# FFN1 by seven products from group 2 on, with left operands stored whole

## The chip, the cores and the metric

The kernel runs on one core of a Trainium2 chip. The metric is the device time of one execution in microseconds. Three runs of the kernel before took 1750.65, 1750.65 and 1752.18 us; their median is 1750.65.

## The reference

One layer of a decoder: a half-step feed-forward block, a mixer of a short convolution and a diagonal state-space model (SSM), and a second half-step feed-forward block, each behind an RMSNorm with shift and scale from a condition vector. Tokens and model width are 1024 each, the feed-forward width is 2816; all in float32.

```python
h = modulate(rms_norm(x, ffn1_norm), sh1, sc1)
x = x + 0.5 * g1 * swiglu(h, w_gate, w_up, w_down)      # (silu(h @ w_gate) * (h @ w_up)) @ w_down
h = modulate(rms_norm(x, mix_norm), sh2, sc2)
...                                                     # conv and SSM, joined by w_out, added to x
h = modulate(rms_norm(x, ffn2_norm), sh3, sc3)
x = x + 0.5 * g3 * swiglu(h, w_gate2, w_up2, w_down2)
y = rms_norm(x, final_norm)
```

## The kernel before

**Products.** Activations lie transposed, a tile being 128 features by 512 tokens (half h of the tokens, feature tile k). Each float32 product is made of three passes (`mm3`): both operands are split into a rounded part `hi` and a rest `lo`, and hi x hi, hi x lo, lo x hi are accumulated in a PSUM bank. A split is a cast on ScalarE (ACT) and a subtraction on VectorE (DVE). Weights come from DRAM as raw tiles of 1 MB (`rawp`, two buffers), are split in pairs of half-columns called granules, and lie in a ring of three granule buffers; `ws.take` hands a granule to the products, and `ws.free` starts the split of a later one.

**FFN1.** The 2816 features are 22 tiles, two to a group, so groups 0 to 10. A group's gate and up projections can be made in two ways. By eight products (`gate_up`), each side and feature tile of each token half takes 8 `mm3`, 64 in all or 192 matmuls. By seven products (`seven`, a Strassen-Winograd scheme), the activation is a 2 by 2 block matrix of token halves and feature halves, A11, A12, A21, A22, and the products use the left operands A11, S1, S2, S3, A12, A22 and S4, where S1 = A21 + A22, S2 = S1 - A11, S3 = A11 - A21 and S4 = A12 - S2. Each side takes seven products of four `mm3`, 56 `mm3` or 168 matmuls for a group. For it GpSimd (POOL) combines the weights' blocks with eight additions for a group (`combine`, `split_done`), and VectorE adds the partial results out of PSUM, five additions for each side. `SEVEN_FROM = (4, 1)` says from which group on this is done in FFN1 and in FFN2.

**Left operands of the projections.** `combos` makes S1, S2 and S3 for each of four k from the split parts of the normalised activation: three whole values are put together again (`whole`, f in the profile), one sum and two differences are made, and the three results are split. `combos_last` makes S4 from two more whole values, once the last plain group is done with A21.

**Left operands of the down projection.** The result a = silu(gate) x up of groups 1 to 8 is used by `down7`, again by seven products, in two chunks of four groups. The seven left operands of each group are made at the end of the group, split (`keep`, `keep_sums`, `keep_last`), and stored as hi and lo together, 512 KB each, to DRAM (`kept`). Groups 0, 9 and 10 keep only their four blocks, for plain products at the end (`last_parts`, fald in the profile). `fetch` brings an operand back, hi and lo, into a buffer that the product before has freed: chunk 0 during the up side of the last group by seven (fa10u), chunk 1 during the second half of the first `down7` (`fad0`; a `down7` has two halves p, of seven steps with two banks each), the last blocks during the second half of the second. FFN2 uses the same functions (fb and fbd in the profile), with groups 1 to 8 kept.

**Side work and order.** A `Clock` counts `mm3` calls. Each `period` calls it runs one step of a generator in `clock.side`. In FFN1 that is `side1`: first `ssm_base` (18 steps: the powers and rotors of the SSM), then `combos` (12), then eight `ssm_batch` (tables for four SSM groups each, stored to DRAM and used in the mixer, with `kp` and `tp` on TensorE). The period is 4 in groups 1 to 3 (3 after `combos_last` is put in front) and 7.75 after. At the start of group 10 what is left of the side work is run at once. Apart from the prologue (`InOrder.strict`), the framework lays down the order of each engine's instructions at compile time; each engine then runs its own list in that order, and a wait at its head holds all behind it. All loads and stores are issued by one queue, SP.

**The x tiles.** `xp` holds x (eight tiles of 512 KB) in the prologue; the normalised x goes through temporary tiles into hi and lo, and `xp` is closed after group 0's first products. x is loaded again at the start of group 10.

Of the kernel before, what the change touches and what calls it, by code (L numbers as in the profile page):

```python
# [21 lines left out]
P = 128  # L22
# [12 lines left out]
SEVEN_FROM = (4, 1)  # L35
# [196 lines left out]
def hymba_layer(ctx: ExitStack, tc, x_d, wm1_d, wmod_d, gu1_d, gs1_d, ds1_d, wl1_d, win_d, wout_d, glu_d, gu2_d, gs2_d, wd2_d, ds2_d, wl2_d, cols_d, cond_d, lam_d, bc_d, out_d):  # L232
# [257 lines left out]
    def keep_sums(kept, a11, a21, a22, name):  # L490

        V.tensor_tensor(out=a22[:], in0=a21[:], in1=a22[:], op=ALU.add)
        keep(kept, "S1", a22, name)
        V.tensor_tensor(out=a21[:], in0=a11[:], in1=a21[:], op=ALU.subtract)
        keep(kept, "S3", a21, name)
        V.tensor_tensor(out=a22[:], in0=a22[:], in1=a11[:], op=ALU.subtract)
        keep(kept, "S2", a22, name)

    def keep_last(kept, a12, s2, name):
        V.tensor_tensor(out=a12[:], in0=a12[:], in1=s2[:], op=ALU.subtract)  # L500
        keep(kept, "S4", a12, name)

    def gu_keep(fi, h, pg, pu, afs, kept, name):
        t = t2k(f"{name}{fi}_{h}")
        A.activation(t[:], pg[:], AF.Silu)
        V.tensor_tensor(out=t[:], in0=t[:], in1=pu[:], op=ALU.mult)
        keep(kept, f"A{h + 1}{fi + 1}", t, name)
        afs[fi, h] = t
        if len(afs) == 4 and "S1" in kept:
            keep_sums(kept, afs[0, 0], afs[0, 1], afs[1, 1], name)  # L510
            keep_last(kept, afs[1, 0], afs[1, 1], name)
# [63 lines left out]
    def seven(name, between, place=1, kept=None, then=None):  # L575
# [4 lines left out]
        for side in "gu":  # L580
# [5 lines left out]
            def out(h, fi, t):  # L586
                nm = f"{name}_{fi}_{h}"
                if side == "g":
                    A.activation(t[:], t[:], AF.Silu)
                    gate_[h, fi] = t  # L590
                else:
                    V.tensor_tensor(out=t[:], in0=t[:], in1=gate_[h, fi][:], op=ALU.mult)
                    if kept is None:
                        a_tiles[fi, h] = split_act(t[:], nm + "a")
                    else:
                        keep(kept, f"A{h + 1}{fi + 1}", t, name)

            for n, (left, b) in enumerate(SEVEN):
# [26 lines left out]
                elif n == 4:  # L625
                    t = gate_[0, 0]
                    V.tensor_tensor(out=t[:], in0=t[:], in1=bank["A"][:], op=ALU.mult)
                    if kept is None:
                        a_tiles[0, 0] = split_act(t[:], f"{name}_0_0a")
                    else:  # L630
                        keep(kept, "A11", t, name)
                elif n == 5:
                    add(u3, u3, "E")
                    out(1, 0, u3)
                    if side == "u" and kept is not None and "S1" in kept:
                        keep_sums(kept, gate_[0, 0], u3, t1, name)
                elif n == 6:
                    add(u2, u2, "C")
                    out(0, 1, u2)
                    if side == "u" and kept is not None and "S1" in kept:  # L640
                        keep_last(kept, u2, t1, name)
# [161 lines left out]
    for k in range(KT):  # L803
        ts = []
# [6 lines left out]
        for h in range(2):  # L811
            hi, lo = parts(f"h1{k}_{h}")
            A.activation(hi, ts[h][:], AF.Identity, bias=sh)
            V.scalar_tensor_tensor(out=lo, in0=ts[h][:], scalar=sh, in1=hi.bitcast(F32), op0=ALU.add, op1=ALU.subtract)
# [13 lines left out]
    xp_open.close()  # L828
# [832 lines left out]
```

## Time and profile before

| | before |
|---|---|
| median of three runs | 1750.65 us |
| span of the profiled execution | 1750.3 us |
| FFN1 groups 1 to 3, by eight products | 87.2 to 219.3 us |
| FFN1 groups 4 to 10, by seven | 219.3 to 505.4 us |
| FFN1 down projection by seven | 505.4 to 669 us |
| FFN2 by seven, groups 1 to 10 | 1153 to 1534 us |
| FFN2 down projection by seven | 1534 to 1686 us |

The profile is of one execution. Its span, from the first to the last instruction, is 0.35 us below the median of the runs. Engines are PE (TensorE matmuls), PEld (its weight loads), DVE, ACT, POOL and the queue SPq. Nearly all instructions are recorded at line 107, that of a helper, so they are told apart by their tiles: `w<-raw` is a weight split, `fa4uC` the bank C of the up side of FFN1's group 4, `rot` and `rott` the rotors. In a table by stage, each engine's busy us are followed by the number of its instructions; then come the granted clock of PE, the busy share of the DMA engines and what they moved in GB/s. In a timeline the columns are start, length, what ran, and in brackets how long the engine had been idle and what released it. A wait is given as total, times and longest.

### The profile page before, as it was taken

Reading aid. Unit: us, or ns where it says so; the run is one execution under the profiler, and the core shown is the slowest. Engines: PE = TensorE matmul, PEld = TensorE weight load, DVE = VectorE, ACT = ScalarE, POOL = GpSimd, SP = SyncE. Lnnn points to the kernel's source line nnn. Section 1 sums busy time; section 2 is a strip of 40 time slices with the busy share of each in tenths; the row PEclk is TensorE's granted clock in tenths of the full one; section 3 lists DMA queues with packets and bytes.
Section 4 is the critical chain, followed back from the end, with each engine's and each line's share of the span. In section 5 each row is a group of like instructions: output and inputs, shape, how many; then the busy total and the mean of one; then the engine's idle time right before and its main releaser. Section 6 shows DMA issues by size and latency. Waiting matters only on the chain.

```text
span 1750.3 us, 20808 instructions
## 1 busy us (share of the span) xinstructions
PE 1677.9 (96%) x7532; PEld 1379.6 (79%) x7532; DVE 1300.6 (74%) x2286; ACT 566.0 (32%) x934; POOL 351.1 (20%) x241
## 2 busy tenths in 40 slices
PE   4999999999999999999999899989999999999996
PEld 3788887878787888887877778778888888888886
DVE  7999999999855687744656977967777666676656
ACT  4223234444322221332113424423343443322221
POOL 0000132222222221100000022023323322333211
PEclk9999999999999999999999999999999999999998
DMA  8245544444597877134654450113444334669312
GB/s 319 85 145 196 207 167 165 182 169 178 196 391 266 326 256 292 56 84 149 210 157 140 144 191 25 48 46 135 157 162 173 147 133 156 239 242 366 115 49 96
DMA packets 101080, 304.54 MB, mean 174 GB/s; under 512 B 19057, under 2 KB 34673, under 8 KB 89842
## 3 DMA queue, kind: packets, MB, share of 16 engines
q1 hardware_dynamic: 100978, 303.22, 48.4%
q8 instruction: 59, 0.97, 0.2%
q14 instruction: 43, 0.35, 0.1%
HBM read 212.47 MB, written 86.51 MB: 171 GB/s over the span
## 4 chain that ended last, share of the span: by engine, by line
PE 76%; DVE 14%; DMA 5%; issue 2%; POOL 1%; ACT 1%; SPq 1%; DVEq 0%; POOLq 0%; ACTq 0%
PE wo L107 4%; PE fald L107 3%; DVE w L107 3%; PE p L107 2%; PE fb10d L107 2%; PE fbd_0B L107 2%; PE fbd_1B L107 2%; PE u L107 2%; DMA swz<-si 2%; PE b L107 1%; DVE x L107 1%; PE c L107 1%; PE fa3u L107 1%; PE fb0g L107 1%; PE fa2g L107 1%
## 5 line engine op out<-in xcount | busy, mean ns | idle before, releaser
L107 ACT CAST w<-raw 128x512 fp32r<-128x512 f32 (+1 forms) x358 | 236.2, 689 | 484.3 <-issue 75.0
L107 DVE TENSOR_TENSOR w<-raw,w 128x512 fp32r<-128x512 f32 (+1 forms) x358 | 295.9, 845 | 107.3 <-ACT w L107 106.5
L164 POOL TENSOR_TENSOR sums<-raw 128x512 f32<-128x512 f32 x50 | 71.4, 1429 | 451.5 <-DMA raw<-in_gs 263.3
L173 POOL TENSOR_TENSOR raw<-sums,raw 128x512 f32<-128x512 f32 x50 | 77.7, 1554 | 371.1 <-DVE w L107 358.9
L175 POOL TENSOR_TENSOR raw<-raw 128x512 f32<-128x512 f32 x50 | 77.5, 1549 | 89.6 <-DVE w L107 73.0
L107 DVE CUSTOM_DVE_ANT_0 wm<-wm,cact 128x1024 f32<-128x1024 f32 x56 | 76.6, 1375 | 16.9 <-DMA wm<-in_wmod 16.9
L165 POOL TENSOR_TENSOR raw<-raw 128x512 f32<-128x512 f32 x50 | 77.3, 1547 | 3.2
L366 POOL TENSOR_TENSOR n3aq<-n3aq,n3aq 128x512 f32<-128x512 f32 x5 | 8.3, 1666 | 281.4 <-DMA wm<-in_wmod 255.7
L107 PE MATMUL p<-h,w 128*128 128x512 f32 x192 | 50.0, 423 | 8.0 <-DVE h L107 5.1
L107 DVE TENSOR_TENSOR w<-sums,w 128x512 fp32r<-128x512 f32 x50 | 52.5, 1063 | 3.6 <-ACT w L107 3.0
L107 PEld LDWEIGHTS p<-h,w 128*128 128x128 f32 x192 | 39.4, 207 | 18.4 <-DVE h L107 6.4
L107 PE MATMUL v<-h,w 128*128 128x512 f32 x192 | 46.9, 395 | 0.0
L107 PE MATMUL c<-h,w 128*128 128x512 f32 x192 | 46.6, 395 | 0.0
L107 PE MATMUL wo<-oa,w 128*128 128x512 f32 x192 | 45.6, 392 | 0.9 <-DVE w L107 0.7
L107 PE MATMUL b<-h,w 128*128 128x512 f32 x192 | 45.6, 394 | 0.0
L107 PE MATMUL wo<-ob,w 128*128 128x512 f32 x192 | 45.5, 392 | 0.0
L107 PE MATMUL u<-h,w 128*128 128x512 f32 x192 | 44.7, 392 | 0.2 <-DVE h L107 0.2
L107 PEld LDWEIGHTS wo<-oa,w 128*128 128x128 f32 x192 | 35.8, 188 | 9.0 <-DVE w L107 1.1
L107 PEld LDWEIGHTS u<-h,w 128*128 128x128 f32 x192 | 35.7, 188 | 8.2 <-DVE h L107 0.6
L107 PEld LDWEIGHTS wo<-ob,w 128*128 128x128 f32 x192 | 35.8, 188 | 7.7 <-DVE ob L107 0.4
L107 PEld LDWEIGHTS b<-h,w 128*128 128x128 f32 x192 | 35.6, 188 | 7.1
L107 PEld LDWEIGHTS c<-h,w 128*128 128x128 f32 x192 | 35.4, 188 | 7.0
(1565 smaller groups left out, 4056.2 us busy)
## 6 DMA issues: line engine op xcount, KB each, us to landing
raw<-in_gs SPq DMA_DIRECT2D x34, 1024.0 KB, 5.5
wm<-in_wmod SPq DMA_DIRECT2D x56, 512.0 KB, 5.3
raw<-in_ds SPq DMA_DIRECT2D x16, 1024.0 KB, 7.2
raw<-in_gu SPq DMA_DIRECT2D x10, 1024.0 KB, 7.0
mw<-in_wm SPq DMA_DIRECT2D x8, 1024.0 KB, 12.8
x<-in_x SPq DMA_DIRECT2D x16, 512.0 KB, 8.0
raw<-in_win SPq DMA_DIRECT2D x8, 1024.0 KB, 5.4
raw<-in_wl SPq DMA_DIRECT2D x5, 1024.0 KB, 6.7
```

Source lines behind the costliest of these rows:

```text
L107: r = getattr(self.engine, name)(*args, **kw)
L164: self.G.tensor_tensor(out=f, in0=r[2], in1=r[1], op=ALU.subtract)
L165: self.G.tensor_tensor(out=r[1], in0=r[1], in1=r[0], op=ALU.subtract)
L173: self.G.tensor_tensor(out=r, in0=s["t3"], in1=r, op=ALU.add)
L175: self.G.tensor_tensor(out=r, in0=self.chunk(j, 3), in1=r, op=ALU.subtract)
L366: nc.gpsimd.tensor_tensor(out=a, in0=a, in1=sq[:, :n], op=ALU.add)
```

## The change

1. `SEVEN_FROM` becomes (2, 1): groups 2 and 3 of FFN1 are made by seven products; their weights come in the order and the combinations of that scheme. Group 1 is then the last by eight.
2. The prologue writes the normalised x (before the shift) over x, and `xp` stays open. `combos1` takes the left sums from there, with the shift added on the way, without putting hi and lo together, and closes `xp` after S4. It runs first in `side1`; `ssm_base` and the batches follow. The small pool `first` is opened behind it.
3. `rotors` makes both tables in one pass: the upper 64 partitions hold what was a second table (`baset` is laid out for this), and a negated copy is made on ACT. Two multiplications and an addition in place of four and two; four stores of half size for the two tables.
4. Kept operands are stored whole, not split: two to a tile of 512 KB (`HALVES`), stored when both are written, so four stores for a group instead of seven. `fetch` brings 256 KB back and splits it then, on ACT and DVE. Sums are read from these tiles, and A21 is stored too. This holds for both FFNs.
5. The clock's periods become 3.5 in group 1, 2 after its second last part, and 7 from group 2 on.

```diff
-SEVEN_FROM = (4, 1)
+SEVEN_FROM = (2, 1)
...
-    def keep(kept, left, src, name):
-
-        if left in kept:
-            t = mov(f"{name}{left}")
-            A.copy(t[:, 0, :], src[:])
-            V.tensor_tensor(out=t[:, 1, :], in0=src[:], in1=t[:, 0, :].bitcast(F32), op=ALU.subtract)
-            SP.dma_start(kept[left][:], t[:].bitcast(F32))
...
+    HALVES = dict(A22=("X", 0), A11=("X", 1), A21=("Y", 0), A12=("Y", 1), S1=("Z", 0), S3=("Z", 1), S2=("W", 0), S4=("W", 1))
...
+        def done(self, left):
+            t, i = HALVES[left]
+            self.there.setdefault(t, set()).add(i)
+            if len(self.there[t]) == 2:
+                SP.dma_start(self.dram[t][:], self.tiles[t][:])
...
+    def keep(kept, left, a, b, op, name):
+
+        V.tensor_tensor(out=kept.place(left, name), in0=a, in1=b, op=op)
+        kept.done(left)
...
     def fetch(kept, left, where, name):
         t = mov(f"{name}{left}", where)
-        SP.dma_start(t[:].bitcast(F32), kept[left][:])
-        return t[:, 0, :], t[:, 1, :]
+        hi, lo = t[:, 0, :], t[:, 1, :]
+        whole_ = lo.bitcast(F32)
+        SP.dma_start(whole_, kept.stored(left))
+        A.copy(hi, whole_)
+        V.tensor_tensor(out=lo, in0=whole_, in1=hi.bitcast(F32), op=ALU.subtract)
+        return hi, lo
...
-            ts.append(t2k(f"h1t{k}_{h}"))
-            V.scalar_tensor_tensor(out=ts[h][:], in0=x[k][h], scalar=scl[:, 0, k : k + 1], in1=bcs[h][:], op0=ALU.mult, op1=ALU.mult)
+            V.scalar_tensor_tensor(out=x[k][h], in0=x[k][h], scalar=scl[:, 0, k : k + 1], in1=bcs[h][:], op0=ALU.mult, op1=ALU.mult)
...
-        def rotors(i, op):
-            r, t = bt(f"rot{b}_{i}"), bt(f"rott{b}_{i}")
-            V.tensor_tensor(out=v3(r), in0=st[0], in1=bs[i], op=ALU.mult)
-            V.tensor_tensor(out=v3(t), in0=st[1], in1=bs[1 - i], op=ALU.mult)
+        def rotors():
+
+            r, t = bt(f"rot{b}"), bt(f"rott{b}")
+            V.tensor_tensor(out=v3(r), in0=st[0], in1=bs[0], op=ALU.mult)
+            V.tensor_tensor(out=v3(t), in0=st[1], in1=bs[1], op=ALU.mult)
             yield
-            V.tensor_tensor(out=r[:, :512], in0=r[:, :512], in1=t[:, :512], op=op)
-            SP.dma_start((co_d, si_d)[i][b], r[:, :512])
-
-        yield from rotors(0, ALU.subtract)
+            V.tensor_tensor(out=r[:, :512], in0=r[:, :512], in1=t[:, :512], op=ALU.add)
+            A.activation(t[64:128, :512], r[64:128, :512], AF.Copy, scale=-1.0)
+            for half in (slice(0, 64), slice(64, 128)):
+                SP.dma_start(co_d[b, half], r[0:64, :512])
+            SP.dma_start(si_d[b, 0:64], r[64:128, :512])
+            SP.dma_start(si_d[b, 64:128], t[64:128, :512])
+
+        yield from rotors()
...
+    def combos1():
...
+        for k in range(4):
+            (t11, t21), (t12, t22) = x[k], x[4 + k]
+            V.scalar_tensor_tensor(out=t22, in0=t22, scalar=both[:, k : k + 1], in1=t21, op0=ALU.add, op1=ALU.add)
+            blocks["S1"].append(split_act(t22, f"h1S1_{k}", "B"))
+            yield
+            V.tensor_tensor(out=t21, in0=t11, in1=t21, op=ALU.subtract)
+            blocks["S3"].append(split_act(t21, f"h1S3_{k}", "B"))
+            yield
+            V.scalar_tensor_tensor(out=t11, in0=t22, scalar=sh[:, k : k + 1], in1=t11, op0=ALU.subtract, op1=ALU.subtract)
+            blocks["S2"].append(split_act(t11, f"h1S2_{k}", "B"))
+            yield
+            V.scalar_tensor_tensor(out=t12, in0=t12, scalar=sh[:, 4 + k : 5 + k], in1=t11, op0=ALU.add, op1=ALU.subtract)
+            yield
+        while not left_free:
+            yield
+        for k in range(4):
+            blocks["S4"].append(split_act(x[4 + k][0], f"h1S4_{k}", "A"))
+            yield
+        xp_open.close()
+        first_opened()
+
     def side1():
+        yield from combos1()
+        sb = side_open.enter_context(tc.tile_pool(name="sb", bufs=1, side="right"))
...
-        yield from combos(act1, "h1", "BBB")
         for b in range(NB):
             yield from ssm_batch(b)
...
-    clock.period = 4
+    clock.period = 3.5
...
-    clock.period = 7.75
+    clock.period = 7
```

More of the change, by code (lines that the diff above doesn't have):

```diff
@@ L634, in seven @@
                     out(1, 0, u3)
-                    if side == "u" and kept is not None and "S1" in kept:
-                        keep_sums(kept, gate_[0, 0], u3, t1, name)
+                    if side == "u" and kept is not None and kept.sums:
+                        keep_sums(kept, name)
                 elif n == 6:
@@ L639, in seven @@
                     out(0, 1, u2)
-                    if side == "u" and kept is not None and "S1" in kept:
-                        keep_last(kept, u2, t1, name)
+                    if side == "u" and kept is not None and kept.sums:
+                        keep_last(kept, name)
                 if q % 2:
@@ L827, in hymba_layer @@
     InOrder.strict = False
-    xp_open.close()
     def kept_for(g, all_seven=True):
-        names = [left for left, _ in SEVEN] if all_seven else ["A11", "A12", "A21", "A22"]
-        return {left: scratch.tile([P, 2, HALF], F32, name=f"kept{g}{left}") for left in names}
+        return Kept(f"kept{g}", all_seven)
     kept = {g: kept_for(g, g not in LAST[0]) for g in range(NGRP)}
@@ L1088, in ssm_batch @@
         yield from gate1()
-        yield from rotors(1, ALU.add)
         yield from gate1()
@@ L1160, in gate_up @@
                     if h:
-                        clock.side.appendleft(combos_last(act, "h1", "A"))
-                        clock.period = 3
+                        left_free.append(True)
+                        clock.period = LAST_PERIOD
                 ws.free(2)
```

86 lines of the change are left out of this document (54 added, 32 removed).

## The prediction

> **What bounds the kernel now.** I read the page's shares first, then a table by stage, the chain of waits in order of time, PE's waits, and last the groups of VectorE and the two places where kept operands come back.
>
> ```profile
> PE 1677.9 (96%) x7532; PEld 1379.6 (79%) x7532; DVE 1300.6 (74%) x2286; ACT 566.0 (32%) x934; POOL 351.1 (20%) x241
> DVE  7999999999855687744656977967777666676656
> ```
>
> TensorE (PE) is busy for 96% of the span, so matmuls taken away are time taken away, unless another engine then ends last. VectorE (DVE) is at 74% on average, but at nine tenths in slices 2 to 10, the stage that the change rewrites. By group of FFN1 (groups 1 to 9; first the wall time, then PE, PEld, DVE, ACT, POOL):
>
> ```profile
> core 0: us, PE busy (x) PEld busy (x) DVE busy (x) ACT busy (x) POOL busy (x), PEclk, DMA share, GB/s
> 87.20:130.72 43.52, 43.52 (x193) 36.07 (x193) 41.94 (x222) 12.17 (x17) 0.00 (x0) 1.00 0.43 146
> ...
> 301.04:340.70 39.66, 39.66 (x181) 32.46 (x181) 37.32 (x59) 15.93 (x29) 11.78 (x9) 1.00 0.50 180
> 340.70:385.00 44.30, 41.73 (x183) 33.51 (x182) 41.14 (x62) 16.37 (x31) 14.53 (x9) 0.96 0.48 171
> ...
> sum 380.07, PE 374.19 PEld 306.45 DVE 358.23 ACT 139.94 POOL 83.17; mean PE 41.58 PEld 34.05 DVE 39.80 ACT 15.55 POOL 9.24
> ```
>
> DVE works 358.23 of 380.07 us: two engines are nearly full at once. The chain shows PE's prices (start, length):
>
> ```profile
> 130.72 10.88 PE fa2g L107 x48
> ...
> 185.12 0.98 PE kp L107 x8
> 186.09 0.59 PE tp L107 x4
> ...
> 219.34 2.72 PE fa4gA L107 x12
> ```
>
> A group by eight products is 192 matmuls, four such pieces, 43.52 us; by seven it is 14 pieces of 2.72, 38.08 us. Groups 1 to 9 need 3 x 43.52 + 6 x 38.08 + 8 x 1.57 (kp and tp of each table batch) = 371.6 us. They took 380.07, so 8.5 us are lost, where PE waits for DVE and then runs for a while at a lower clock (0.96 in the row from 340.70):
>
> ```profile
> PE fa7gC L107 <- DVE fa7gt L107: 2.6, 1, 2.6
> PE fa5uC L107 <- DVE fa5ut L107: 2.1, 1, 2.1
> PE fa9gC L107 <- DVE fa9gt L107: 1.2, 1, 1.2
> ```
>
> **The change part by part.** *Groups 2 and 3 by seven products*: 2 x 5.44 = 10.9 us of PE gone. I take all of it, if DVE leaves room, which is the next sum.
>
> ```profile
> L107 DVE TENSOR_TENSOR w<-raw,w 128x512 fp32r<-128x512 f32 x75 | 54.5, 747 | 5.5 <-ACT w L107 5.4
> L107 DVE TENSOR_TENSOR rot<-rot,rott 128x512 f32<-128x512 f32 x16 | 16.0, 1001 | 0.2
> L107 DVE TENSOR_TENSOR rott<-rs,rt 128x512 f32<-128x512 f32 x16 | 15.3, 959 | 2.1 <-DMA co_d<-rot 2.1
> L107 DVE TENSOR_TENSOR rot<-rs,rt 128x512 f32<-128x512 f32 x16 | 14.2, 885 | 0.1
> L107 DVE TENSOR_TENSOR w<-raw,w 128x1024 fp32r<-128x1024 f32 x10 | 12.2, 1218 | 0.0
> L107 DVE TENSOR_TENSOR f<-h 128x512 f32<-128x512 f32 x16 | 10.9, 688 | 0.1
> L107 DVE TENSOR_TENSOR fa1S<-fa,fa1S 128x512 fp32r<-128x512 f32 x4 | 2.8, 689 | 0.0
> L107 DVE TENSOR_TENSOR fa4A<-fa4gc,fa4A 128x512 fp32r<-128x512 f32 x1 | 1.8, 1780 | 0.0
> L107 DVE TENSOR_TENSOR fa4gu<-fa4gt,fa4gB 128x512 f32<-128x512 f32 x1 | 0.7, 669 | 0.0
> ```
>
> DVE in groups 1 to 9: each of the two groups adds 10 additions from PSUM (0.67) and turns 4 wide weight splits (1.22) into 14 narrow ones (0.75): 6.7 + 10.5 - 4.9 = 12.3, so +24.6. The left sums take 4 whole-tile operations for each of four k instead of 9, as the whole values are in x's place: 20 fewer x 0.69 = -13.8. Rotors halved: half of 16.0 + 15.3 + 14.2 = -22.7. Stores kept whole: seven splits fewer in each of groups 1 to 8 and four in group 9, 60 x 0.69 = -41.4. The sum is 358.2 + 24.6 - 13.8 - 22.7 - 41.4 = 305 us in 371.6 - 10.9 = 360.7 us of PE: 85% instead of 94%.
>
> That is an average, so by stage. A group by seven without side work is seen in FFN2:
>
> ```profile
> 1191.35:1229.42 38.07, 38.07 (x169) 31.54 (x169) 26.81 (x40) 15.29 (x27) 11.56 (x8) 1.00 0.42 152
> 1495.98:1534.06 38.08, 38.08 (x170) 31.55 (x169) 21.38 (x30) 13.33 (x23) 12.48 (x9) 1.00 0.74 275
> 1534.06:1572.10 38.04, 38.04 (x170) 31.51 (x169) 27.46 (x35) 10.22 (x18) 11.04 (x8) 1.00 0.62 250
> 1572.10:1610.20 38.10, 38.10 (x170) 31.58 (x169) 25.21 (x34) 9.17 (x16) 10.74 (x8) 1.00 0.86 323
> 1610.20:1648.30 38.10, 38.10 (x170) 31.57 (x169) 25.85 (x31) 9.17 (x16) 14.57 (x10) 1.00 0.44 174
> ```
>
> It has 26.8 us of DVE, 22.0 without its seven splits (7 x 0.69). Group 1 now gets the left sums: 32 operations x 0.69, 8 products and sums x 0.69, some 6 us of weights: 34 of 43.5 us. The period gives 13 + 8 side steps there and the sums need 20, so S4 stands just before group 2. Groups 2 and 3 get the table base: it cost 41.94 less 15 x 0.69 and 5 x 1.22, 25.5 us, in group 1's 16 steps; now 8 steps to a group, 12.8, so 34.8 of 38.1 us, the tightest place. Groups 4 to 9 get 4/3 of a batch each: (37.32 - 26.81 - 2.8 for rotors) x 4/3 = 10.3, so 32.3 of 40.2. Stalls should mostly go; groups 2 and 3 at 91% keep some. Of the 8.5 us I take 5.5 as won (bounds 0 and 8.5).
>
> *Fetching*. A kept operand comes back as 256 KB instead of 512, and ACT's cast and DVE's subtraction now stand behind its landing, 28 of each for a chunk, in both FFNs: a full block of ACT 28 x 0.62 (the casts' price, the same width as the weights') and of DVE 28 x 0.69 = 19.3 us. Behind a cast that waits for its DMA are ACT's weight casts and t1 copies, and PE waits for those weights; behind the subtraction are DVE's bank evacuations. In FFN2 PE has no idle time there at all today. Chunk 0 falls into the last 15 us of group 10 and into the first half (1534 to 1572): 21.4 + 27.5 + 19.3 = 68.2 of 76.1 us, though most of it lands around the seam. Chunk 1 falls into 1572 to 1610: 25.2 + 19.3 = 44.5 us of DVE against 38.1 of PE, 6.4 over, paid back in the next half, which has 12 us free. PE feels it only if a weight or a bank is late. That margin is thin:
>
> ```profile
> 1597.44 0.41 SPq L107 DMA_DIRECT2D raw<-in_ds  x1
> ...
> 1607.21 0.62 ACT L107 CAST w<-raw 128x512 fp32r<-128x512 f32 x1 [1.15 <-DMA raw<-in_ds]
> 1609.08 1.77 DVE L107 TENSOR_TENSOR w<-raw,w 128x512 fp32r<-128x512 f32 x1
> ```
>
> The split at 1609.08 serves a product that starts at 1610.2. Its raw tile landed ten us after issue, in a stage at 323 GB/s: 3.2 MB, 1 MB of it the raw tile itself. Halving the rest saves 1.1 MB, 3.4 us, which pays half of the 6.4. I take +5 us for FFN2, from 0 (backlog absorbed) to +14: 6.4, and 4 at the seam, with the slow clock after each stall.
>
> FFN1 has the same added work, but a loss to win back:
>
> ```profile
> 505.40:543.50 38.10, 38.03 (x168) 31.19 (x166) 23.52 (x35) 8.26 (x15) 2.15 (x3) 1.00 0.93 346
> 543.50:590.00 46.50, 42.71 (x169) 33.85 (x170) 26.76 (x33) 10.18 (x19) 16.66 (x12) 0.93 0.74 281
> 532.98 1.28 SPq L107 DMA_DIRECT2D raw<-in_ds  x2
> 543.07 0.62 ACT L107 CAST w<-raw 128x512 fp32r<-128x512 f32 x1 [14.26 <-DMA raw<-in_ds]
> ```
>
> The half from 543.50 takes 46.50 instead of 38.1, 8.4 lost, because the next weights were issued only at 532.98, behind fetches that fill the queues (share 0.93), and landed ten us later. 28 x 256 KB less is 7.3 MB, 21 us at 346 GB/s, so they come earlier. Against this stands the same +5. I take -2 (bounds -8.4 and +14).
>
> *At nothing*: stores of four 512 KB tiles instead of seven (DMA share is 0.42 to 0.50 there; the tile is held until both its halves are written, and four buffers serve four tiles); the new groups' two copies and narrower casts, and the rotors' negation, on ACT, which works 15.93 of 39.66 us; x written in place. The weight bytes are the same. The rotors' stores are four for each batch instead of two; si's lower half waits on SP for ACT's negation, and behind it on SP are weight loads, which run two tiles ahead. Without that cover it is about 1 us (0.62 and an issue of 0.41) for each of eight batches. The tables move about a group and a half later; the last batch's stores now stand on SP at the end of group 9, ahead of the reload of x, which x's first use, in the seam's half, is 38 us behind; if it came late, the whole of that delay would show at 505.
>
> Sum: -10.9 - 5.5 + 5 - 2 = -13.4 on the profiled execution's 1750.3, so 1736.9; the runs' median is 0.35 above that execution, so **1737 us**.
>
> The row of 1780 ns is a price of its own: the same subtraction takes 0.69 elsewhere, and the slow ones stand where POOL is busy. [...] It speaks against this change, which adds such GpSimd work.
>
> **The rivals.** *A, the fetch costs more than the seven products win.* DVE and ACT stand behind landings in order, and the backlog isn't absorbed: 10.4 us (6.4 and 4) in each FFN, some 13 with the slow clock, and FFN1's relief lost: -16.4 + 26 = +9.6, **1760**. It decides the sign from 8 us for each FFN on. For it: 44.5 against 38.1 us, and a split with 1.1 us to spare. Against: half the bytes, and 12 us free in the next half. 0.2.
>
> *B, DVE becomes the bound of groups 2 and 3.* Each now has eight POOL combinations, as 1191.35 shows, beside the table base. If each blocks DVE for 1.78 - 0.69 = 1.09 us, 34.8 + 8.7 = 43.5 us: as long as before, nothing won by the products. -5.5 + 5 - 2 = -2.5, **1748**. Against: the 26.81 already holds eight such collisions. [...] 0.15.
>
> *C, fetching is hidden altogether*: -10.9 - 8.5 - 8.4 + 0 = -27.8, **1723**. For it: DMA was FFN1's limit there; against: the 6.4 over. 0.12.
>
> **How the numbers follow.** The forecast has 0.53, with its own range 1729 to 1746. Two runs of this kernel tell apart about 0.2%, 3.5 us: faster is below 1747, slower above 1754. Faster: 0.53 + 0.12 + a third of B, 0.7; same: the rest of B, 0.1; slower: A, 0.2. For eight in ten the range leaves half of A and half of C outside: 1726 to 1757.
>
> **What would show it.** Groups 2 and 3 at 38.1 us plus at most 2 each; DVE below 0.9 in groups 4 to 9 and PE's waits for fa5ut, fa7gt, fa9gt gone; the half after the seam of FFN1 near 41 instead of 46.5; in FFN2 PE idle of 2 to 4 us in the seam or the half from chunk 1. I am wrong if groups 2 and 3 exceed 41 us (B), if FFN2's four halves together grow by over 8 us (A), or not at all (C).

## The result, and the profile after

The changed kernel takes 1789.95 us (median of four runs, 1786.33 to 1793.41) beside 1751.41 for the kernel before: ratio 1.0226 [1.0211, 1.0241]. I had forecast 1737. The profiled execution has a span of 1788.5 us.

The engines' shares of the page, and VectorE's slices:

```profile
PE 1709.1 (96%) x7484; PEld 1370.8 (77%) x7484; DVE 1304.4 (73%) x2282; ACT 584.6 (33%) x968; POOL 383.1 (21%) x257
DVE  7939999889688997635557967965555555699846
```

PE has fewer matmuls than before and is busy for 31 us more. VectorE falls to three tenths in the third slice, group 1 of FFN1, and is at nine in those behind it. By stage (the columns are those of the prediction: wall time, the engines, clock, DMA): FFN1's groups 1, 2, 3 and 6, the two halves of its first down product, and a group of FFN2 that the change doesn't touch:

```profile
86.34:130.82 44.48, 44.48 (x193) 36.05 (x192) 16.38 (x21) 9.29 (x16) 8.51 (x6) 1.00 0.27 95
130.82:177.54 46.72, 40.95 (x169) 32.46 (x168) 44.65 (x184) 16.88 (x32) 9.57 (x8) 0.93 0.25 82
177.54:224.65 47.11, 41.50 (x169) 33.03 (x168) 46.31 (x168) 16.18 (x24) 12.99 (x9) 0.93 0.31 108
...
307.10:348.34 41.24, 41.00 (x181) 32.46 (x180) 35.90 (x52) 13.13 (x23) 13.11 (x9) 1.00 0.43 146
...
515.18:554.38 39.20, 39.20 (x169) 31.52 (x168) 36.44 (x53) 17.04 (x30) 16.84 (x8) 1.00 0.61 215
554.38:593.58 39.20, 39.20 (x169) 31.52 (x168) 34.84 (x49) 20.07 (x35) 12.10 (x9) 1.00 0.65 219
1208.98:1248.18 39.20, 39.20 (x169) 31.54 (x168) 21.34 (x33) 11.46 (x20) 11.95 (x8) 1.00 0.29 108
```

Two things are to be seen. The last row is a group by seven products in which PE never waits and has full clock, and it takes 39.20 us instead of 38.07. And groups 2 and 3 take 47 instead of 38, with VectorE full (44.65 of 46.72) and the clock down, while in group 1 VectorE works only 16.38 of 44.48 us. PE's waits (total, times, longest):

```profile
PE fa2uC L107 <- DVE fa2ut L107: 5.8, 1, 5.8
PE fa3uC L107 <- DVE ro_r L107: 5.6, 1, 5.6
PE fa10uC L107 <- DVE fa10ut L107: 2.0, 1, 2.0
PE fad_0A L107 <- DVE w L107: 1.9, 1, 1.9
PE fb10uC L107 <- ACT fb1lA L107: 1.8, 1, 1.8
```

(A releaser is named by the instruction that ended last. In the waits of fa2uC, fa3uC and fb10uC PE starts 0.15 us after VectorE's addition that empties the bank, `fa2ut<-fa2uu,fa2uC` and its like; the `ro_r` and the `fb1lA` of these rows are other operations that ended in between.)

The first row of the stages is the clue to the larger part: group 1, by eight products in both kernels, has 192 matmuls at full clock without a wait, in 44.48 us instead of 43.52. PE's timeline in FFN2 says the same for each product. After:

```profile
1329.38 2.96 PE L107 MATMUL fb5gC<-h3S,w 128*128 128x512 f32 x12
1332.18 2.96 PE L107 MATMUL fb5gB<-h3S,w 128*128 128x512 f32 x12
```

Before:

```profile
1321.74 2.88 PE L107 MATMUL fb5gC<-h3S,w 128*128 128x512 f32 x12
1324.46 2.88 PE L107 MATMUL fb5uA<-h,w 128*128 128x512 f32 x12
```

Each length holds the modelled end of the last matmul; from start to start it is 2.80 us for 12 matmuls instead of 2.72, or 233.3 ns for one instead of 226.7.

### The profile page after: what moved, and what is told of

Same layout as the page of the kernel before. It is cut to its first block, busy times and chain, and to the rows that moved or that the text cites. A ratio compares the mean times of both kernels' runs of the same rounds, so it can differ in the third digit from the quotient of the medians.

```text
span 1788.5 us, 20702 instructions
## 1 busy us (share of the span) xinstructions
PE 1709.1 (96%) x7484; PEld 1370.8 (77%) x7484; DVE 1304.4 (73%) x2282; ACT 584.6 (33%) x968; POOL 383.1 (21%) x257
## 4 chain that ended last, share of the span: by engine, by line
PE 66%; DVE 11%; DMA 4%; issue 1%; ACT 1%; POOL 0%; SPq 0%; DVEq 0%; ACTq 0%; POOLq 0%
PE wo L107 4%; PE fald L107 3%; PE fb10d L107 2%; PE b L107 2%; DVE w L107 2%; PE u L107 2%; PE fbd_1B L107 2%; PE fbd_0B L107 2%; DMA swz<-si 2%; DVE x L107 1%; PE fbd_0A L107 1%; PE fad_1B L107 1%; PE fb0g L107 1%; PE fbd_1C L107 1%; PE fbd_1A L107 1%
## 5 line engine op out<-in xcount | busy, mean ns | idle before, releaser
L107 ACT CAST w<-raw 128x512 fp32r<-128x512 f32 (+1 forms) x374 | 241.3, 677 | 578.9 <-issue 66.4
L107 DVE TENSOR_TENSOR w<-raw,w 128x512 fp32r<-128x512 f32 (+1 forms) x374 | 302.4, 828 | 139.5 <-ACT w L107 138.9
L173 POOL TENSOR_TENSOR raw<-sums,raw 128x512 f32<-128x512 f32 x54 | 82.2, 1521 | 460.3 <-DVE w L107 449.8
L164 POOL TENSOR_TENSOR sums<-raw 128x512 f32<-128x512 f32 x54 | 78.7, 1458 | 351.3 <-DMA raw<-in_gs 175.2
L175 POOL TENSOR_TENSOR raw<-raw 128x512 f32<-128x512 f32 x54 | 91.7, 1701 | 91.4 <-DVE w L107 91.4
L165 POOL TENSOR_TENSOR raw<-raw 128x512 f32<-128x512 f32 x54 | 84.2, 1559 | 4.2
L107 ACT CAST w<-sums 128x512 fp32r<-128x512 f32 x54 | 32.7, 621 | 36.9 <-PE fa2uA L107 4.5
```

What stands on the lines that cost most here:

```text
L107: r = getattr(self.engine, name)(*args, **kw)
L164: self.G.tensor_tensor(out=f, in0=r[2], in1=r[1], op=ALU.subtract)
L165: self.G.tensor_tensor(out=r[1], in0=r[1], in1=r[0], op=ALU.subtract)
L173: self.G.tensor_tensor(out=r, in0=s["t3"], in1=r, op=ALU.add)
L175: self.G.tensor_tensor(out=r, in0=self.chunk(j, 3), in1=r, op=ALU.subtract)
```

## The experiments

### What changed the pace of all matmuls

What is common to all of PE's work and differs between the kernels is where the operands lie. The change adds a constant, `both`, of four columns, to the right-hand side of the memory, where pools are stacked downward from the end; it takes 32 bytes, and everything behind it (the weight ring, raw tiles, x) lies 32 bytes lower. The weight ring starts on a multiple of 256 bytes before (202752, 210944, 219136) and 32 below one after. The left-hand side, with the tiles that PE streams against the weights (`movA`, from 1536), is where it was. Both sides begin with a padding tile of `PAD` columns of 4 bytes.

**a_aligned**: the changed kernel, with the padding on the right cut by the 32 bytes.

```diff
-PAD = 96, 96
+PAD = 96, 88
```

> The changed kernel with the right-hand padding tile 32 bytes smaller, so that the 32 bytes of its new constant tile `both` no longer shift the weight ring, the raw tiles and the temporaries below it. Theory S (shift): the twelve matmuls of a product take 2.72 us again instead of 2.80, some 7000 matmuls x 6.7 ns = 47 us come back, and the kernel takes about 1744 us (1739 to 1750). Rival D (the new engine balance, its stores, fetches or order slow PE's pace): the product stays at 2.80 us and the time within 3 us of 1790.

It took 1757.28 us, ratio 1.0038 [1.0020, 1.0057], and 12 matmuls 2.72 us. 32 of the 38.5 us are gone, not the 47 that I had expected; what is left is in the next part.

**b_shift32, b_ring32, b_rest32**: the kernel before, with all of the right-hand side 32 bytes down (`PAD = 96, 104`); with the ring alone (a tile of 32 bytes ahead of the ring, one of 224 behind it); with all but the ring (a tile of 32 bytes behind the ring's pool).

> The kernel before with the right-hand padding tile 32 bytes larger and nothing else changed: the ring, raw tiles and temporaries lie as in the changed kernel. Theory S: a product takes 2.80 us instead of 2.72, and the time rises by some 7050 matmuls x 6.7 ns = 47 us to about 1798 us. Rival D: nothing changes, 1751 us and 2.72 us.

> The kernel before with only the weight ring shifted by 32 bytes (a 32-byte tile ahead of it, one of 224 bytes behind it, so that all else stays on multiples of 256 bytes). If the weights' own address sets the pace: 2.80 us for a product, about 1798 us. If it is that of the raw tiles, the temporaries or x, which other engines read beside PE: 2.72 us and 1751 us.

> The kernel before with the raw tiles, temporaries, tables and x shifted by 32 bytes and the weight ring left where it was. If the weights' own address sets the pace: 2.72 us for a product and about 1751 us. If it is the address of what VectorE, ScalarE and GpSimd read: 2.80 us and about 1798 us.

They took 1781.01 (two runs), 1781.29 and 1750.22 us (one run each). The ring's place alone does it, without any other part of the change. The loss is 31 us and not the expected 47. About half of the difference lies in groups 1 to 9 of FFN1, where VectorE's part of the waits shrinks while PE is slower: they take 383.29 us in b_shift32 instead of 380.07, 3.2 more, where 6.6 ns for each of their 1,681 matmuls would be 11 (group 7 takes 43.52 us there, in the kernel before 45.62).

**b_shift64, b_left32, b_both32, b_same32**: the kernel before with `PAD = 96, 112`, `104, 96`, `104, 104` and `104, 88`.

> The kernel before with 64 bytes more in front of the right-hand pools, so that the weight ring lies 64 bytes short of a multiple of 256 (remainder 192) instead of on one. If the pace asks only for a multiple of 64, 12 matmuls take 2.72 us and the time stays at 1750; if it asks for more (128 or 256), they take 2.80 and the time is about 1781. I take the first as the likelier, 0.6.

> The kernel before with 32 bytes more in front of the left-hand pools, which hold the moving operands (movA); the weight ring stays on multiples of 256. If only the weights' address sets the pace of a matmul, 12 matmuls take 2.72 us and the time stays at 1750; if the moving operand's address does so too, 2.80 and about 1781. I take the first as the likelier, 0.7.

> The kernel before with 32 bytes more in front of the left-hand pools (moving operands) and of the right-hand pools (weight ring), so that both are shifted against a multiple of 256 (remainders 32 and 224). If each operand has to start on a multiple of its own, the two shifts add up or stay: 12 matmuls take 2.80 us or more, and the time is 1781 or above. If only the distance of the two counts, it would have to be a multiple of 64 here (their sum of shifts is 64 bytes), and 12 matmuls take 2.72 to 2.75 us, the time 1750 to 1764. I take the first as the likelier, 0.65.

> The kernel before with the left-hand pools (moving operands) and the weight ring both 32 bytes up from a multiple of 256: each is off its multiple by what b_left32 and b_ring32 shifted alone, but their distance is unchanged. If the distance of the two operands sets the pace, 12 matmuls take 2.72 us and the time is 1750; if each address counts for itself, 2.80 us or more and 1781 or above. After b_both32 (distance 64 bytes: 2.745 us as in b_shift64) I take the distance, 0.85.

| version | moving operand, mod 256 | ring, mod 256 | an FFN2 group, us | 12 matmuls, us | time, us |
|---|---|---|---|---|---|
| before | 0 | 0 | 38.08 | 2.72 | 1750.42 |
| b_rest32 | 0 | 0 | 38.08 | 2.72 | 1750.22 |
| b_same32 | 32 | 32 | 38.08 | 2.72 | 1751.39 |
| b_shift64 | 0 | 192 | 38.45 | 2.75 | 1764.25 |
| b_both32 | 32 | 224 | 38.45 | 2.75 | 1759.70 |
| b_ring32 | 0 | 224 | 39.20 | 2.80 | 1781.29 |
| b_shift32 | 0 | 224 | 39.20 | 2.80 | 1781.01 |
| b_left32 | 32 | 0 | 39.20 | 2.80 | 1781.53 |

(The group is from start to start of FFN2's group 2; 12 matmuls are a fourteenth of it. The time of before is a median of ten runs, that of b_shift32 of two; the others are of one run each, so they rest on the pace in the trace as well.) b_shift64, b_left32 and b_both32 came out against what I held likelier. It isn't the address of either operand: it is their distance. At a multiple of 256 bytes a matmul takes 226.7 ns, at 64 bytes off 228.9, at 32 bytes off 233.3; b_same32, with both operands off, is as fast as before. Only these three distances were tried, the ring always on the same side of the moving operand, so which multiples are enough, and what other distances cost, stays open. PE's timeline of b_same32 and of b_ring32:

```profile
1321.00 2.88 PE L107 MATMUL fb5gC<-h3S,w 128*128 128x512 f32 x12
1323.72 2.88 PE L107 MATMUL fb5uA<-h,w 128*128 128x512 f32 x12
```

```profile
1322.56 2.96 PE L107 MATMUL fb5gA<-h,w 128*128 128x512 f32 x12
1325.36 2.96 PE L107 MATMUL fb5gC<-h3S,w 128*128 128x512 f32 x12
```

### What the rest of the change does

With the pace restored, a_aligned shows the change itself. By stage: group 1, 2, 3, 4 to 9; then the halves of FFN1's first down product.

```profile
84.87:128.39 43.52, 43.52 (x193) 36.04 (x192) 16.52 (x21) 9.41 (x17) 8.53 (x6) 1.00 0.28 97
128.39:177.87 49.48, 41.02 (x170) 32.94 (x168) 48.58 (x191) 16.88 (x32) 10.91 (x8) 0.90 0.26 84
177.87:223.23 45.36, 40.48 (x170) 33.01 (x168) 44.32 (x159) 16.13 (x24) 11.37 (x8) 0.92 0.30 105
223.23:469.84 246.61, 243.21 (x1106) 198.19 (x1104) 224.07 (x365) 82.16 (x145) 73.64 (x48) 0.99 0.48 161
509.92:548.00 38.08, 38.08 (x170) 31.54 (x168) 36.15 (x54) 17.38 (x30) 16.59 (x7) 1.00 0.62 222
548.00:586.08 38.08, 38.08 (x170) 31.55 (x168) 35.20 (x49) 20.05 (x35) 12.78 (x10) 1.00 0.67 225
```

Against the kernel before (both by the starts of the products in the profiled execution, spans 1755.5 and 1750.3): the prologue is 2.2 us shorter; groups 1 to 9 take 384.97 instead of 380.07, 4.9 more; group 10 and FFN1's down products 262.7 instead of 268.8, 6.1 less; the mixer with FFN2's first groups 1.5 more; FFN2's group 10 and first down product 4.3 more, what follows 2.7 more. That is +5.1 of the spans' +5.2 (the medians lie 6.9 apart).

**a_four**: parts 3 and 4 of the change alone.

```diff
-SEVEN_FROM = (2, 1)
+SEVEN_FROM = (4, 1)
...
-        yield from combos1()
+        yield from ssm_base(sb1)
+        yield from combos(act1, "h1", "BBB")
```

> The kernel before with parts 3 and 4 of the change alone: rotors halved, operands of the down projections stored whole and split when they are fetched, in both FFNs. Seven products begin at group 4 as before, order and periods of the side work are as before, and there is no tile 'both', so the weight ring lies where it did before (12 matmuls in 2.72 us). Theory (what costs the aligned kernel its 8.9 us against the forecast and more is the table base falling into groups 2 and 3; the stores, rotors and fetches do about what I summed): groups 1 to 9 take 372 to 376 us instead of 380.07, FFN1's down projection keeps its gain of about 6 us, FFN2 its loss of about 4: 1743 us, between 1738 and 1748. Rival (storing whole and splitting at the fetch is itself the loss): 1752 or more.

1747.13 us, ratio 0.9981 [0.9968, 0.9994]; in the profiled execution, of 1744.21 us, groups 1 to 9 take 371.68 us, and PE never waits in them. FFN1's down products (262.7 with group 10 in a_aligned) take 264.6, FFN2's group 10 40.08. Groups 1 to 9 of a_four and of a_aligned:

```profile
86.42:458.10 371.68, 371.68 (x1681) 305.38 (x1680) 303.34 (x641) 114.75 (x191) 82.77 (x54) 1.00 0.45 154
```

```profile
84.87:469.84 384.97, 368.24 (x1634) 300.19 (x1632) 333.50 (x733) 124.58 (x218) 104.43 (x70) 0.97 0.41 138
```

Parts 1, 2 and 5 (seven products in groups 2 and 3, the sums first, the tables next) take 13.3 us more instead of 10.9 less between these two executions (the medians lie 10.2 apart), and VectorE works 30 us more.

**a_late**: a_aligned with the base spread, by the period, over groups 2 to 4.

```diff
+        clock.period = 9.33 if g < 5 else 5.83
         seven(f"fa{g}", lambda: None, kept=kept[g], ...
```

> The aligned kernel after (a_aligned) with one change: the side work's period is 9.33 in groups 2 to 4 and 5.83 in groups 5 to 9 instead of 7 throughout, so the 16 steps of the table base spread over three groups instead of two, and the table batches crowd into five. Theory (VectorE is over-filled in groups 2 and 3 by the base): groups 2 and 3 lose less, 49.5 + 45.4 becomes 82 to 88 us, group 4 takes 40 to 43, the later ones 0 to 1 each more; total 1747 us, between 1743 and 1754. Rival (groups 2 and 3 are slow through the seven products' own work there, the combinations on GpSimd or the weights' order): they stay near 95 us together and the total at 1757 or above.

1761.96, 1.0060 [1.0037, 1.0084]. Groups 2 and 3 take 42.25 and 52.04 us, together 94.3 instead of 94.8, group 5 46.17. The period hardly spaces the base: its first operation runs at 140.6 us instead of 138.9 and its last at 237.2 instead of 228.4, so it takes 97 us instead of 90, where the periods' ratio would make 119. In an order laid down beforehand by what is ready, a generator's steps run when their data and their memory are there, not only when the clock calls them; in the kernel before, the base began at 69 us, ahead of the group that calls it.

**a_ring**: a_aligned with the ring's fourth buffer given up earlier.

```diff
+    ws.retire(ring1)
     afs = {}
...
-    ws.retire(ring1)
     pro_open.close()
```

> The aligned kernel after (a_aligned) with one line moved: the ring's fourth weight buffer is retired before group 0's last products instead of behind them, so that no weights of group 1 lie in it. In a_aligned its last weights there (w7) are read until the end of group 1, 128.39 us, and the memory of the left sums S1 to S3 lies over it; their 12 splits stand behind that and come in one burst from 129.29, x is free only then, and the whole table base, whose tiles lie in x's place, falls into groups 2 and 3. Theory: with the fourth buffer gone the splits run early in group 1, where VectorE works 15.8 of 43.0 us, the base begins in group 1, and VectorE's work of groups 2 and 3 falls by some 15 us: the waits for w in fa2uC (8.5) and ro_r in fa3uC (4.9) go, groups 2 and 3 together take 78 to 85 us instead of 94.8, total 1744 us, between 1739 and 1750. Rival (the base's amount, wherever it starts, is what over-fills groups 2 and 3, or the loss is in the seven's own work): groups 2 and 3 together above 90, total 1754 or more.

1752.59, 1.0018 [1.0006, 1.0030]. The 12 splits now run early in group 1, the base begins at 116 us instead of 139, and VectorE works 29.3 of 43.5 us there. But group 2 takes 49.66 us, as in a_aligned, group 3 40.06, and group 4 44.00: 4.7 us won, against the 13 expected. The earlier start empties group 3, not group 2: counted by its tiles, overlaps once, the base takes 8.1 us of VectorE in group 1, 31.5 in group 2 and 12.2 in group 3, where a_aligned has 0, 26.0 and 25.3. Its share alone doesn't set a group's time: in a_ring_split2 group 3 has 13.7 us of it and takes 45.33. No run takes a part of the base away.

**a_split2, a_ring_split2, a_four_split2**: FFN2's operands split at the store and fetched as hi and lo, as before the change.

```diff
+            SP.dma_start(t[:].bitcast(F32), kept[left][:])
+            return hi, lo
```

> The aligned kernel after (a_aligned) with FFN2's operands split at the store and fetched as hi and lo, as before; FFN1 keeps whole stores. Theory (ACT's cast and VectorE's subtraction behind the landing are what delays fb10uC and fbd_0A): group 10 of FFN2 returns from 42.05 to 38.1 us, the first half of its down projection from 76.5 to 76.2, total 4.3 us less than a_aligned: 1753. Rival (the wait comes from the order of the loads): FFN2 stays as in a_aligned, total 1757.

> a_ring with FFN2's operands split at the store and fetched as hi and lo, as before (the edit of a_split2). If the two parts are independent, the 2 to 4 us that a_split2 won come on top: 1741 us, between 1736 and 1747, faster than the kernel before by some 9 us. If a_ring gains nothing, 1753.

> a_four (seven products from group 4 on as before, rotors halved, whole stores) with FFN2's operands split at the store and fetched as hi and lo. a_four was 2.5 us faster than before, with FFN2's group 10 at 40.08 us instead of 38.08 and the first half of its down projection at 76.99 instead of 76.16: this returns 2 to 3 us, 1744 us, between 1741 and 1748. Compared with a_ring_split2 it shows what the seven products in groups 2 and 3 are worth by themselves once their side work fits: 10.9 us by the count of matmuls less what stalls they bring; by my theory a_ring_split2 is the faster by 2 to 8 us, by the rival it is slower.

1755.14 (1.0021 [1.0004, 1.0039]), 1747.62 (0.9984 [0.9975, 0.9994]) and 1742.92 (0.9955 [0.9938, 0.9971]): 2 to 5 us less than without the edit. FFN2's group 10 returns to 38.08 us in all three. a_four_split2 beats both kernels, by 7.7 us beside before's 1750.6, and a_ring_split2, with the seven products in groups 2 and 3, is 4.7 slower than it, against my theory, by which it was to be the faster: there the products don't pay, in any version that I ran.

**a_zero, a_ring_split2_zero**: the 56 stores of zeros for the tables, which `ssm_base` issues, taken out of it and put behind group 0 (the tile goes to the constants and takes 512 bytes, so the distance stays on a multiple of 256).

```diff
+    zero = const.tile([CH, 128], F32, name="zero")
...
-        zero = sb1.tile([CH, 112], F32, name="zero")
```

> The aligned kernel after (a_aligned) with the 56 stores of zeros that the table base issues taken out of it: they are issued from a constant tile of 512 bytes (which leaves the operands' distance on a multiple of 256) behind group 0's first products, where they ran in the kernel before. In a_aligned 23 of them hold the load queue from 146.4 to 161.1 us, the next raw weights are issued only at 161.24, land at 167, and PE waits 8.5 us in fa2uC. Theory (the stores moved past the weight loads are what group 2 loses; VectorE's load is what group 3 and later lose): that wait goes, group 2 takes 38 to 42 us instead of 49.5; part of it comes back as VectorE's waits in groups 2 and 3; total 1749 us, between 1745 and 1753. Rival (VectorE's order and load would hold fa2uC anyway): group 2 stays above 45, total 1754 or more.

> a_ring_split2 with the same edit as a_zero. There no weight is late behind the zero stores; PE's waits in groups 2 and 3 (3.9 for fa2gt, 4.1 for fa3gt) are on VectorE, whose work in groups 2 and 3 stays as it is. Theory: groups 2 and 3 together stay at 88 to 93 us, total 1746 us, between 1743 and 1749, so that a_four_split2 (1742.9) stays the fastest. Rival (the queue's stores were behind these waits too): groups 2 and 3 below 85, total 1741 or less.

1757.87 (1.0044 [1.0024, 1.0063]) and 1751.32 (1.0007 [0.9992, 1.0023]): nothing won in a_zero, and in the second 3.7 us lost beside a_ring_split2, of which I have no account. In a_zero group 2 takes 49.03 us, and PE waits 8.0 us in fa2uC again, so the rival came: VectorE holds fa2uC. The chain behind that wait, in a_aligned's timeline (start, length, what; in brackets the idle time before and its releaser):

```profile
129.29 7.31 DVE L107 TENSOR_TENSOR h1S<-x,h1S 128x512 fp32r<-128x512 f32 x12
...
153.11 2.88 PE L107 MATMUL fa2uB<-h1S,w 128*128 128x512 f32 x12
153.97 1.14 ACT L107 CAST w<-raw 128x512 fp32r<-128x512 f32 x2
...
158.56 0.68 DVE L107 TENSOR_TENSOR w<-raw,w 128x512 fp32r<-128x512 f32 x1
159.26 0.68 DVE L107 TENSOR_TENSOR w<-raw,w 128x512 fp32r<-128x512 f32 x1
...
161.24 0.52 SPq L107 DMA_DIRECT2D raw<-in_gs  x1
...
165.25 0.69 DVE L107 TENSOR_TENSOR fa2uu<-fa2ut,fa2uB 128x512 f32<-128x512 f32 x1
...
167.17 1.29 POOL L164 TENSOR_TENSOR sums<-raw 128x512 f32<-128x512 f32 x1 [19.76 <-DMA raw<-in_gs]
168.43 1.31 POOL L173 TENSOR_TENSOR raw<-sums,raw 128x512 f32<-128x512 f32 x1
...
170.99 0.67 DVE L107 TENSOR_TENSOR fa2uu<-fa2uu,fa2uD 128x512 f32<-128x512 f32 x1
...
171.79 0.67 DVE L107 TENSOR_TENSOR fa2ut<-fa2uu,fa2uC 128x512 f32<-128x512 f32 x1
172.39 0.18 DVE L107 TENSOR_TENSOR w<-ro_r 128x32 f32<-128x32 f32 x1
...
172.61 5.46 PE L107 MATMUL fa2uC<-h1S,w 128*128 128x512 f32 x12 [8.46 <-DVE w L107]
```

ACT has cast the weights by 155; VectorE subtracts them only at 158.56 and 159.26, behind the base's small operations, and the next raw tile is issued at 161.24 and lands at 167. But this tile is not what PE waits for: VectorE splits it at 173.98, when PE has already started. PE's last product of the group goes into bank C, which VectorE's addition of 171.79 has to empty first; it ends at 172.46, and PE starts 0.15 us later (in a_zero 172.69 and 172.84). The `w` in the bracket is a small tile of the base that has the same name as the weights and was written in between. PE had filled bank B by 156, and VectorE adds it at 165.25, in the order of its list: it works 32.98 of the 33.67 us from 138.93 to 172.60, some 24 of them on the base. In a_zero the raw tile is issued 0.4 us earlier, at 160.87, and the wait stays. So neither the stores nor the load hold PE here, but VectorE's list, in which the sums stand behind the base.

And beside POOL the base is slow:

```profile
167.16 0.18 DVE L107 TENSOR_TENSOR r<-ro_r 128x32 f32<-128x32 f32 x1
167.26 1.25 DVE L107 TENSOR_TENSOR r<-ro_i 128x32 f32<-128x32 f32 x1
...
168.54 1.25 DVE L107 TENSOR_TENSOR r<-ro_r,ro_i 128x32 f32<-128x32 f32 x1
```

The same kind of operation takes 0.18 us if it starts before POOL's instruction of 167.17, and 1.25 under it, ending as POOL's ends (168.46), and again under the next. The trace shows what I didn't see in the prediction: an instruction of 0.18 us lost 1.07 us there, about as much as one of 0.69 in the kernel before, which lost 1.09 (1.78 at 259.0 us, under a POOL instruction from 258.53 to 260.21).

**a_paced, a_paced_v**: a_ring_split2, with each step of the base held behind the instructions that stand before it in the program, on all engines and on VectorE alone.

```diff
+    def paced(steps):
+        while True:
+            InOrder.strict = True
...
-            yield from ssm_base(sb, sb1)
+            yield from paced(ssm_base(sb, sb1))
```

> a_ring_split2 with one addition: each of the table base's steps is held behind the VectorE instructions that stand before it in the program, so that the clock's period really spaces the base out over groups 2 and 3; in the other versions its instructions run as soon as their data is there, one step after another. Theory (the base came in one block ahead of the sums that PE waits for): the waits for fa2gt and fa3gt (3.9 and 4.1 us) shrink to below 2 each, groups 2 and 3 together take 80 to 87 us instead of 92.5, total 1740 us, between 1735 and 1746. Rival (it is the amount: the base's small instructions beside GpSimd's combinations are more than fits, however they are spaced): groups 2 to 4 together stay at 132 to 136 us and the total at 1747 or above.

> a_paced with the base's steps held back on VectorE alone; in a_paced they were held on ScalarE and the load queue too, and PE waited 14.9 us once for a weight in group 5. Theory left by a_paced (the base's amount beside GpSimd's combinations over-fills groups 2 and 3, spacing helps little): that one wait goes, groups 2 and 3 together take 86 to 92 us, total 1744 to 1751. Rival (spacing does it, and only the other two queues spoiled it): groups 2 to 4 together below 125 us instead of 134.5, total 1741 or less.

1765.98 (1.0093 [1.0075, 1.0111]) and 1765.62 (1.0105 [1.0070, 1.0140]). Groups 2 and 3 take 89.0 and 93.2 us together instead of 92.5, so holding the base back brings 3.5 in the one and nothing in the other; the rest is lost in groups 4 and 5 (103.0 and 98.6 instead of 81.7). Holding the other queues wasn't the reason for that, as I had thought; the load queue and ScalarE of a_paced_v show it:

```profile
228.78 36.72 SPq L108 DMA_DIRECT2D mk_d<-zero  x56
265.61 0.51 SPq L108 DMA_DIRECT2D raw<-in_gs  x1
...
271.00 0.62 ACT L108 CAST w<-raw 128x512 fp32r<-128x512 f32 x1 [25.11 <-DMA raw<-in_gs]
```

The zeros belong to the base's last step, and when that is held back, all 56 stores stand in one block of 36.72 us ahead of the next weights. A version that paces the base and takes the zeros out was not tried, so what pacing alone is worth stays open.

## Why the prediction was wrong, step by step

**"x written in place" and the rest, at nothing: the step that failed first.** Under this heading I costed what the new edits do and not where they lie. The four columns of `both` moved the weight ring against the moving operands: 1789.95 less 1757.28 is 32.7 us, and b_shift32 shows 31 without the change. Added to the forecast, that alone turns the sign; so does the second step alone, as a_aligned is still 6.9 us slower than the kernel before. No row of the kernel before shows it, as the operands of its products all lie at a distance of a multiple of 256 bytes; the two padding tiles at the heads of both sides were there to be asked about. At 6.6 ns for each of 7,484 recorded matmuls it would be 49 us; in groups 1 to 9 it is only 2.3 (387.31 against 384.97), as PE waits for VectorE there anyway.

**"25.5 us, in group 1's 16 steps; now 8 steps to a group, 12.8": the second failed step.** Three things were wrong in it. Its size: I took what VectorE did in group 1 for the whole base, but it had begun in the prologue. The rows of one of its tables in the kernel before and in a_aligned (count, ns min/median/max, first and last start):

```profile
L107 DVE TENSOR_SCALAR tab<-pw x36: 136/174/307, 70.5 to 98.4; 64x32 f32<-64x32 f32 x32, 64x288 f32<-64x288 f32 x4
```

```profile
L107 DVE TENSOR_SCALAR tab<-pw x36: 164/176/1275, 139.9 to 165.0; 64x32 f32<-64x32 f32 x32, 64x288 f32<-64x288 f32 x4
```

It starts at 70.5, and group 1 at 87.2. Added up by its tiles in the trace, the base is 297 instructions of 195 ns, 58 us, from 69 to 132; operations follow each other closer than they last, so VectorE is busy with it for 40.4 us, overlaps counted once, 27.8 of them in group 1. Its price: POOL did nothing in group 1 of the kernel before; beside it the same 297 instructions take 248 ns on average, and VectorE is busy with them for 53.5 us, 26.0 in group 2 and 25.3 in group 3, where I had 12.8 in each. Its place: the tiles lie where x lies, so nothing of it can start before S4, and then it doesn't keep to eight steps a group (a_late).

**Group 1, "34 of 43.5 us"**: 16.5. The sums, ready early, ran in the prologue (68 to 80 us), and 12 of the splits only at 129.29, because two of their buffers lie on weights that are read until group 1 ends (a_ring). So VectorE's work of groups 1 to 9 was 333.5 us instead of 305, and little of it where there was room.

**The products, -10.9, and the stalls, -5.5**: a_four gives the stalls' -8.4, all of the 8.5, where VectorE works 303.3 of 371.7 us (I had 294 for these parts: 358.2 - 22.7 - 41.4). With the products in groups 2 and 3, a_aligned has +4.9 in place of -16.4. The matmuls went, and waits of 8.5, 4.9 and 3.2 us with a slow clock behind them came. The signs that I had named failed there: groups 2 and 3 above 41. Rival B was the right kind, VectorE beside POOL in groups 2 and 3, and had 43.5 us where 49.5 and 45.4 came. Its price of a collision fits (1.09 us; the operations of 0.18 us lose 1.07). That each of the eight combinations of a group pays it was an estimate: in the row from 1191.35 of the kernel before, which I took to hold eight collisions, two subtractions are that long (1.67 and 1.78 us). The sum also stood on the same 12.8 us of base.

**Fetching, +5 and -2.** FFN2's loss was 7.0 (4.3 and 2.7) with the range from 0 to 14, and the first part is where I said, in the seam, as a bank that VectorE empties behind the subtractions:

```profile
1527.76 1.78 DVE L107 TENSOR_TENSOR fb3lS<-fb3lS 128x512 fp32r<-128x512 f32 x1
...
1529.46 1.74 DVE L107 TENSOR_TENSOR fb4lS<-fb4lS 128x512 fp32r<-128x512 f32 x1
...
1531.13 0.67 DVE L107 TENSOR_TENSOR fb10ut<-fb10uu,fb10uC 128x512 f32<-128x512 f32 x1
...
1531.95 4.29 PE L107 MATMUL fb10uC<-h3S,w 128*128 128x512 f32 x12 [2.45 <-ACT fb1lA L107]
```

The addition that empties bank C ends at 1531.81, 0.15 us before PE starts; the cast of fb1lA only ended in between. The two fetched operands ahead of it take 1.78 and 1.74 us instead of 0.69, as POOL works from 1527.37 to 1530.66: with 0.69 each, some 0.3 of the 2.45 would be left (an estimate).

FFN1's was -6.1: the half behind the seam takes 38.08 us (I had 41, before 46.50), its DMA share 0.67 instead of 0.74 and that of the half before it, in which the fetches run, 0.62 instead of 0.93. So the 8.4 us there came back whole, as half the bytes would make it, and group 10 lost 2.0. The mechanisms were right, the sizes off by 2 and 4. Rival A's 13 us for each FFN did not come.

**The operands' stores and the rotors' at nothing**: PE waits for none of them in a_four. But the step that was moved also issues 56 stores of zeros, which I left out; they cost nothing here (a_zero), and a wait of 14.9 and 11.1 us where the order put them in one block (a_paced, a_paced_v).

**The range** ended at 1757, where a_aligned lies, with the second failed step alone; the first adds to it, and no rival had a price that falls on nearly every matmul.

## What to carry to other kernels

A new constant is an edit to every tile that is stacked behind it (32 bytes cost 31 us in b_shift32): compare the addresses of the two matmul operands before and after, and compare the time of a stage that the change doesn't touch, before looking at the stages that it does. A moved block of work must be priced by all of its instructions, wherever the order had let them start, and at the price that its new neighbours set (here 248 ns an instruction beside POOL instead of 195). A step costs its place from the moment that its memory is free, not from the moment that the program calls it (a_ring's base began at 116 us instead of 139). And the name of a releaser is to be checked against the times: two tiles of one name point here at a load that nobody waited for.

## What the hardware showed that I had not expected

The pace of a matmul (float32 by passes of 128x128 on 128x512) depended on the distance of the two operands' addresses in these runs: 226.7 ns at a multiple of 256 bytes, 228.9 at 64 off, 233.3 at 32 off. Why, these runs do not show.

PE's clock fell after short waits in a_aligned: 12 matmuls behind the wait of 2.45 us took 4.29 instead of 2.88 (granted clock 0.67 from 1531.95 to 1536.00), behind the one of 8.46 us 5.46 (0.50 from 172.61 to 177.70).
